# An early gather with more row buffers, and one tile's rows computed one stage earlier

## The chip, the cores and the metric

The kernel runs on one core of a Trainium2 chip. The time is the device time of one execution in microseconds. TensorE (PE) multiplies matrices, VectorE (DVE) and ScalarE (ACT) work on tiles of 128 partitions, GpSimd (POOL) does elementwise work and issues the indirect loads, SyncE (SP) issues plain loads. Each engine runs its own instructions strictly in the order in which they stand in its queue.

## The reference, cut to what matters

One layer of a decoder on 1024 prompt tokens and 64 sample tokens (8 sequences of 8), width 1024:

```python
xn = rmsnorm(h, norm_mix)
mix = token_mixers(xn, ...)            # one projection, retention heads and RWKV-7 heads, one output projection
h = h + mix
h = h + peer(rmsnorm(h, norm_ffn), peer_wq, peer_keys, peer_u, peer_v)
gate = sigmoid(rmsnorm(h, ple_norm) @ ple_gate)
h = h + gate * (p_l @ ple_proj)
```

`peer` is the part that the change is about. For each token it forms 8 query heads, scores two sets of 128 keys for each, takes the 16 best of each set and the 16 best sums, which gives 128 expert numbers out of 16384 and a softmax over each head's 16. Then

```python
hval = einsum('pd,phkd->phk', xb, u_tab[e])        # 128 rows of 1024 values for each token
act = gelu(hval) * gsm
y = einsum('phk,phkd->pd', act, v_tab[e])          # and 128 rows of the second table
```

All values are float32.

## The kernel before, in words

The 1088 tokens are nine tiles: 0 to 7 are the prompt, 128 tokens each, and 8 is the sample group, 64 tokens. The tiles differ in how `peer` is computed. Tiles 4 to 7 go through all 16384 experts densely (matmuls against both tables, with gates that are zero for experts not chosen). Tiles 0, 1 and 8 (`E0`) and 2 and 3 (`G1`) gather the chosen rows instead: for each of the 128 choices one indirect load fetches one row of 4 KB for each of the 128 partitions (the 64 tokens of tile 8 take two choices at a time), POOL issues it, and DVE works it off. In the first phase (table `pu`, line 1156) DVE multiplies the fetched rows with the token's row and sums them to one number; in the second (table `pv`, line 1170) it adds the scaled rows to a sum that is held in PSUM. In all there are 576 loads of each phase.

The stages, in the order of the program:

1. Projections of tiles 0 and 1 (group A0), then of 2 and 3 (group A1), beside the token mixing of tile 0.
2. Projections of tiles 4 to 8 (group A2). Here the early work begins: the output projection and norm of tile 0 (`c_rows`), its query (`early_query`), its choice of experts (`topk`) and its gather.
3. `group_b`: the token mixing of tiles 1, 8, 2, ..., 7, a chain of small matmuls, DVE and ACT steps, with the `c_rows` of the finished tiles and steps of the early work (queries and gathers of tiles 1 and 8) put between.
4. The handover: `c_rows` of the last tiles, the loads of the rows of tiles 2 to 7 and their transposes (`rows_in`, tile `cx`), then the queries of tiles 2 to 7 (`c_query`). What is left of the early gather runs on.
5. Choice of experts and gates of tiles 4 to 7 (`topk`, `gates`), beside 96 of the 128 blocks of the first dense product (`hidden`). The gathers of tiles 2 and 3 begin.
6. The dense product: the last 32 blocks fused, then the 96 stored ones.
7. The last part (`ple`): per-layer embedding, gate and final norm of tiles 0, 1, 8, 4, 5, 6, 7, 2, 3, in this order.

The order on each engine is set when the kernel is compiled: a scheduler takes the instructions in the program's order as their priority, runs a model of the engines' time, and places what is ready and comes first. So a gather that is late in the program stands early in an engine's queue where that model saw the engine free. Buffers bear a tag and a number of copies; a new tile of a tag waits until the oldest copy has been read.

The early work has one pool, `early`, laid out with the tags `V` (2 copies), `W` and `xy` (1 each), `Wq` (QB = 4) and `xT` (1), each 4 KB per partition. The rows of a gather take the tags of the tuple `rows` in turn, by `rows[j % len(rows)]` in `fetch`, so its length is the number of loads that can be under way or waiting for DVE. Before the change tiles 0 and 1 use `("V", "V", "W", "xy")`, four copies, and tile 8 uses these and `xT`, five. `Wq` holds the weight tiles of the queries of tiles 1 and 8, and at the end the second half of tile 7's mixed values (`tail`, line 984). Tiles 2 and 3 have a pool of their own (`grow`, five copies), which, with the buffers of the gates, lies where the early pool lay, and so waits for the end of the early gather.

Of the kernel before, what the change touches and what calls it, by code (L numbers as in the profile page):

```python
# [8 lines left out]
F32 = mybir.dt.float32  # L9
# [8 lines left out]
D = 1024  # L18
# [144 lines left out]
GBUF = 5  # L163
# [14 lines left out]
E0 = [0, 1, 8]  # L178
# [8 lines left out]
IB = 2  # L187
# [8 lines left out]
QB = 4  # L196
# [17 lines left out]
class K:  # L214
# [485 lines left out]
    def rw_mix(self, t):  # L700
        nc, I, O, wp = self.nc, self.I, self.O, self.cw
# [170 lines left out]
        V = toks["vtk"]  # L872
# [108 lines left out]
        p = self.ps("pgt", PGT or hb[0])  # L981
        nc.tensor.matmul(p[:n], sf13[:, :n], self.g2, start=True, stop=True)
        if t == 7:
            self.tail = self.ep0.tile([128, 512], F32, name="tail", tag="Wq", bufs=QB)
            nc.vector.tensor_tensor(self.tail, xf, p, op=OP.mult)
        else:
            nc.vector.tensor_tensor(xf[:n], xf[:n], p[:n], op=OP.mult)
            nc.scalar.dma_start(self.od[t][:n, 512:], xf[:n])
# [140 lines left out]
            nc.vector.tensor_scalar(e1[:n, 1], ei[:n], 127, None, op0=OP.bitwise_and)  # L1129
            nc.scalar.activation(self.e12[t][:n], e1[:n], AF.Copy)  # L1130

    def gather(self, gp, t, rows=("grow",), parts=1, acc=None):


        nc, I = self.nc, self.I
        n = SIZE[t]
        slot = lambda name, tag: gp.tile([128, D], F32, name=name, tag=tag, bufs=GBUF if len(rows) == 1 else 1 + (tag == "V"))
        home = lambda: acc.tile([128, 2, 512], F32, name="gacc", bufs=1).rearrange("p a b -> p (a b)")

        def fetch(src, j):  # L1140
# [20 lines left out]
        nc.scalar.activation(ac, hv[:, 0], AF.Gelu)  # L1161
        nc.vector.tensor_tensor(ac, ac, self.gsm[t], op=OP.mult)
        y = home()
        for j in range(n):
            g = fetch(I['pv'], j)
            for c in cs:
                if j == 0:
                    nc.vector.tensor_scalar(y[:, c], g[:, c], ac[:, 0:1], None, op0=OP.mult)
                else:
                    nc.vector.scalar_tensor_tensor(y[:, c], g[:, c], ac[:, j:j + 1], y[:, c], op0=OP.mult, op1=OP.add)  # L1170
            if j < n - 1:
                yield j
# [53 lines left out]
    def early(self, wp):  # L1226

        rows = ("V", "V", "W", "xy")
# [8 lines left out]
                yield  # L1237
        yield from g
        for t in E0[1:]:
            yield from self.gather(wp, t, rows + ("xT",) * (t == E0[-1]), acc=self.acc)  # L1240

    def gates(self, wp, t, extra):
        nc = self.nc
# [199 lines left out]
    def build(self):  # L1443
        PS = bass.MemoryType.PSUM
        run = lambda g: [None for _ in g]
        sb = lambda name, es, **kw: self.pool(name, es=es, reuse_waits="tile", **kw)
        with self.es:
# [15 lines left out]
            m = mix[0]  # L1463
            self.interleave(m, 1, a, IA)
            a = self.group_a(pools, A1, "b")
            self.interleave(m, IB, a, 1)
            e1.close()
            e0.close()
            self.ep0 = ep0 = sb("early", ee, side="right")
# [1 line left out]
            early = self.behind(self.early(ep0), PE_)  # L1471
            co = self.co = sb("co", ew, side="right")
            a = self.group_a(self.a_pool(e2, "2"), A2, "b")
            for _ in self.c_rows(co, E0[0]):
                next(a, None)
            for _ in a:
                for _ in range(IE):
                    next(early, None)
# [98 lines left out]
```

## Time and profile before

| | us |
|---|---|
| median of three runs | 3794.01 |
| lowest and highest | 3787.25 and 3801.23 |
| the profiled execution | 3785.29 |
| span of its trace | 3783.5 |

| engine | busy us | share of the span |
|---|---|---|
| PE | 3297.9 | 87% |
| DVE | 2964.3 | 78% |
| POOL | 2374.5 | 63% |
| ACT | 1227.5 | 32% |

The shares are means over stages with different limits, so they are read stage by stage. The profile's page cuts the span in 40 slices and gives each engine's busy share in tenths, the clock that PE was granted, and what the 16 DMA engines moved. The other views used below give the busy time of each engine in chosen stretches, who waited for whom, and single instructions in order of time.

### The profile page before, as it was taken

The numbers are of one execution on the slowest core, as the hardware profiler recorded it, in microseconds if no ns is written. First come the engines' busy times: TensorE is split into PE (matmuls) and PEld (weight loads), VectorE is DVE, ScalarE is ACT, GpSimd is POOL, SyncE is SP. The second block draws the span as 40 slices with busy tenths as digits, with TensorE's granted clock in tenths as the row PEclk, the third lists the DMA queues.
The fourth block names the chain that finished last, engine by engine and source line by source line (L and its number), as shares of the span: only waits on it lengthen the run. The fifth ranks groups of instructions, "written<-read, shape, count | busy, mean of one in ns | idle before, by whom it ended". The sixth has DMA issues, their size and how long they took to land. (4 is left out here: it accounts for less than half of the span.)

```text
span 3783.5 us, 52729 instructions
## 1 busy us (share of the span) xinstructions
PE 3297.9 (87%) x17749; PEld 2733.3 (72%) x17749; DVE 2964.3 (78%) x5858; ACT 1227.5 (32%) x2273; POOL 2374.5 (63%) x2059
## 2 busy tenths in 40 slices
PE   7799995858769978983999999999999989999979
PEld 7698994645648857762887777778788867777857
DVE  4454488978897798886998988997677878788886
ACT  4232221111112111211232635888433333333322
POOL 5363176445364456554559888775788778887752
PEclk9799995668867567876999999999999999999989
DMA  7266568889777878888779889898999999999984
GB/s 256 77 228 218 168 198 286 281 291 315 261 247 271 318 266 276 291 282 320 225 234 320 302 301 311 302 338 339 326 343 336 345 363 376 383 367 359 344 274 145
DMA packets 429898, 1086.24 MB, mean 287 GB/s; under 512 B 46972, under 2 KB 146042, under 8 KB 424955
## 3 DMA queue, kind: packets, MB, share of 16 engines
q0 software_dynamic: 165888, 604.05, 45.5%
q1 hardware_dynamic: 205406, 382.77, 30.9%
q10 hardware_dynamic: 58332, 96.03, 6.8%
q8 instruction: 141, 2.31, 0.3%
q14 instruction: 131, 1.07, 0.1%
HBM read 986.68 MB, written 95.94 MB: 286 GB/s over the span
## 5 line engine op out<-in xcount | busy, mean ns | idle before, releaser
L1142 POOL DMA_INDIRECT grow<-in_pv,eid x576 | 578.5, 1004 | 482.1 <-DVE gacc L1170 292.2
L1142 POOL DMA_INDIRECT grow<-in_pu,eid x576 | 569.7, 989 | 390.5 <-DVE grow L1156 213.4
L1170 DVE SCALAR_TENSOR_TENSOR gacc<-grow,ac,gacc 128x1024 f32<-128x1024 f32 x571 | 731.2, 1281 | 68.4 <-DMA grow<-in_pv,eid 63.4
L1156 DVE SCALAR_TENSOR_TENSOR grow<-grow,gacc 128x1024 f32<-128x1024 f32 x576 | 690.9, 1211 | 103.2 <-DMA grow<-in_pu,eid 101.2
L1317 PE MATMUL py<-ah,vh 128*128 128x512 f32 x1024 | 403.7, 396 | 29.2 <-ACT vh L299 29.0
L328 PE MATMUL ph<-cx,uh 128*128 128x512 f32 x1024 | 409.5, 400 | 21.3 <-ACT uh L299 14.9
L329 PE MATMUL ph<-cx,uh 128*128 128x512 f32 x1024 | 406.5, 397 | 0.0
L1318 PE MATMUL py<-al,vh 128*128 128x512 f32 x1024 | 402.0, 393 | 1.6 <-DVE al L301 1.6
L303 POOL TENSOR_TENSOR vl<-vraw,vh 128x640 fp32r<-128x640 f32 (+2 forms) x224 | 326.3, 1462 | 36.6 <-ACT vh L299 27.3
L303 POOL TENSOR_TENSOR ul<-uraw,uh 128x1024 fp32r<-128x1024 f32 x128 | 308.6, 2412 | 62.7 <-ACT uh L299 32.6
L1320 PE MATMUL py<-ah,vl 128*128 128x512 f32 x1024 | 270.9, 396 | 9.7 <-POOL vl L303 9.5
L331 PE MATMUL ph<-cx,ul 128*128 128x512 f32 x1024 | 261.1, 394 | 8.3 <-POOL ul L303 8.1
L1317 PEld LDWEIGHTS py<-ah,vh 128*128 128x128 f32 x1024 | 193.4, 189 | 81.1 <-ACT vh L299 38.8
L299 ACT ACTIVATE vh<-vraw 128x640 fp32r<-128x640 f32 (+2 forms) x224 | 154.8, 692 | 291.2 <-DMA vraw<-in_pvd 112.3
L328 PEld LDWEIGHTS ph<-cx,uh 128*128 128x128 f32 x1024 | 195.2, 191 | 67.6 <-ACT uh L299 20.7
L1320 PEld LDWEIGHTS py<-ah,vl 128*128 128x128 f32 x1024 | 191.8, 189 | 59.0 <-POOL vl L303 18.0
L1324 DVE TENSOR_TENSOR yT<-yT,py 128x512 f32<-128x512 f32 x216 | 147.3, 684 | 102.8 <-PE py L1320 101.2
L331 PEld LDWEIGHTS ph<-cx,ul 128*128 128x128 f32 x1024 | 189.7, 188 | 50.7 <-POOL ul L303 12.5
L1318 PEld LDWEIGHTS py<-al,vh 128*128 128x128 f32 x1024 | 193.5, 189 | 44.3 <-DVE al L301 2.9
L329 PEld LDWEIGHTS ph<-cx,uh 128*128 128x128 f32 x1024 | 194.9, 190 | 39.2
L299 ACT ACTIVATE uh<-uraw 128x1024 fp32r<-128x1024 f32 x128 | 135.4, 1058 | 188.8 <-DMA uraw<-in_puT 142.4
L303 POOL TENSOR_TENSOR wl<-wraw,wh 128x1024 fp32r<-128x1024 f32 x45 | 116.4, 2586 | 115.4 <-ACT wh L299 95.6
(402 smaller groups left out, 7456.4 us busy)
## 6 DMA issues: line engine op xcount, KB each, us to landing
uraw<-in_puT SPq DMA_DIRECT2D x128, 512.0 KB, 4.3
vraw<-in_pvd SPq DMA_DIRECT2D x152, 320.0 KB, 6.1
cw<-in_w_out SPq DMA_DIRECT2D x128, 256.0 KB, 5.1
wd<-wst ACTq DMA_DIRECT2D x28, 1024.0 KB, 17.7
wt<-wd SPq DMA_DIRECT2D x64, 448.0 KB, 7.1
wraw<-in_w_ret SPq DMA_DIRECT2D x48, 512.0 KB, 4.9
ewq<-in_wq SPq DMA_DIRECT2D x48, 512.0 KB, 7.3
gd<-geh ACTq DMA_DIRECT2D x96, 256.0 KB, 6.0
```

The costliest lines, as they stand in the source:

```text
L299: nc.scalar.activation(hi, src, AF.Copy)
L303: nc.gpsimd.tensor_tensor(lo, src, hi.bitcast(F32), op=OP.subtract)
L328: mm(out, lh(k), rh(k), start=first and k == 0, stop=False)
L329: mm(out, *((ll(k), rh(k)) if right else (lh(k), rl(k))), start=False, stop=False)
L331: mm(out, *((lh(k), rl(k)) if right else (ll(k), rh(k))), start=False, stop=last and k == nk - 1)
L1142: nc.gpsimd.indirect_dma_start(out=g, out_offset=None, in_=src, in_offset=bass.IndirectOffsetOnAxis(ap=self.eid[t][:, j:j + 1], axis=0))
L1156: nc.vector.scalar_tensor_tensor(g[:, c], g[:, c], 1.0, x[:, c], op0=OP.mult, op1=OP.mult, accum_out=hv[:, i, j:j + 1])
L1170: nc.vector.scalar_tensor_tensor(y[:, c], g[:, c], ac[:, j:j + 1], y[:, c], op0=OP.mult, op1=OP.add)
L1317: nc.tensor.matmul(p, vh[:, b, :], ah, start=b == 0, stop=False)
L1318: nc.tensor.matmul(p, vh[:, b, :], al, start=False, stop=False)
L1320: nc.tensor.matmul(p, vl[:, b, :], ah, start=False, stop=b == nb - 1)
L1324: nc.vector.tensor_tensor(yT[:, d, :], yT[:, d, :], p, op=OP.add)
```

## The change

Four edits. First, the rows of the second phase of tile 1's gather also take the four copies of `Wq` (8 in the ring), and tile 8's gather takes them in both phases, with `xT` (9 in the ring). Second, `tail` moves from `Wq` to `xT`, since `Wq` now belongs to the gather. Third, `c_rows` of tile 0 is no longer stepped at the start of group A2, but follows tile 0's mixing beside group A1, with a pool of its own (`co1`). Fourth, for that the two generators are joined in `then`.

```diff
@@ in rw_mix
         if t == 7:
-            self.tail = self.ep0.tile([128, 512], F32, name="tail", tag="Wq", bufs=QB)
+            self.tail = self.ep0.tile([128, 512], F32, name="tail", tag="xT")
@@ in gather
-    def gather(self, gp, t, rows=("grow",), parts=1, acc=None):
+    def gather(self, gp, t, rows=("grow",), parts=1, acc=None, more=()):
-        slot = lambda name, tag: gp.tile([128, D], F32, name=name, tag=tag, bufs=GBUF if len(rows) == 1 else 1 + (tag == "V"))
+        slot = lambda name, tag: gp.tile([128, D], F32, name=name, tag=tag, bufs=GBUF if len(rows) == 1 else dict(V=2, Wq=QB).get(tag, 1))
...
         y = home()
+        rows = rows + more
         for j in range(n):
             g = fetch(I['pv'], j)
@@ in early
         for t in E0[1:]:
-            yield from self.gather(wp, t, rows + ("xT",) * (t == E0[-1]), acc=self.acc)
+            if t == E0[-1]:
+                rows = rows + ("Wq",) * QB + ("xT",)
+            yield from self.gather(wp, t, rows, acc=self.acc, more=("Wq",) * QB if t != E0[-1] else ())
@@ in build
-            self.interleave(m, IB, a, 1)
+            e3 = ExitStack()
+            co = sb("co1", e3)
+
+            def then():
+                yield from m
+                yield from self.c_rows(co, E0[0])
+
+            self.interleave(then(), IB, a, 1)
+            e3.close()
...
             a = self.group_a(self.a_pool(e2, "2"), A2, "b")
-            for _ in self.c_rows(co, E0[0]):
-                next(a, None)
```

The scheduler then places many instructions anew. No engine gets an instruction more or less. Three places follow, on DVE each time; `grow` is a fetched row, `gacc` the sum in PSUM, so lines 1156, 1170 (1171 after the change) are the gather's.

In the last third of group A2's projections (`fdst` is the token shift of a projected block, `eid` the chosen experts of tile 0) there stood before:

```order
L559 SCALAR_TENSOR_TENSOR fdst<-fdst,vec,rs 128x64
L536 COPY rb<-shl 128x1
L541 COPY rs<-shiftT 128x8
L1099 TENSOR_REDUCE ef<-eq 128x16
L301 TENSOR_TENSOR wl<-wraw,wh 128x1024
L555 COPY shl<-rb 128x1
L1123 CAST eid_64<-ef 128x128
L560 COPY shl<-rs 128x8
L554 SCALAR_TENSOR_TENSOR fdst<-fdst,vec,rb 128x512
L559 SCALAR_TENSOR_TENSOR fdst<-fdst,vec,rs 128x64
```

and now, where the first of these blocks is shifted:

```order
L403 TENSOR_SCALAR gsig<-gsig 64x256
L1156 SCALAR_TENSOR_TENSOR grow,hv<-grow,gacc 128x1024
L404 TENSOR_TENSOR retd<-pret,gsig 64x256
L1156 SCALAR_TENSOR_TENSOR grow,hv<-grow,gacc 128x1024 x2
L301 TENSOR_TENSOR wl<-wraw,wh 128x1024
L555 COPY shl<-rb 128x1
L560 COPY shl<-rs 128x8
L1156 SCALAR_TENSOR_TENSOR grow,hv<-grow,gacc 128x1024
L554 SCALAR_TENSOR_TENSOR fdst<-fdst,vec,rb 128x512
L559 SCALAR_TENSOR_TENSOR fdst<-fdst,vec,rs 128x64
```

The experts of tile 0 were chosen between the fourth and fifth block; now the gather runs from the first block on. From the fifth block to the middle of tile 7's mixing, 8 to 18 more fetched rows, mostly 15, have been worked off ahead of each other DVE instruction than before.

At the handover (`ch` is the residual of `c_rows`, here of tile 7, `cx` the transposed rows of the tiles) there stood before:

```order
L301 TENSOR_TENSOR cx_13040<-ntr,cx_13039 128x4x128 x2
L1170 SCALAR_TENSOR_TENSOR gacc<-grow,ac,gacc 128x1024 x5
L609 TENSOR_TENSOR ch<-ewo,ch 128x512 x2
L1170 SCALAR_TENSOR_TENSOR gacc<-grow,ac,gacc 128x1024 x4
L629 SCALAR_TENSOR_TENSOR ch<-ch,crs,cgr 128x512 x2
L1170 SCALAR_TENSOR_TENSOR gacc<-grow,ac,gacc 128x1024
L301 TENSOR_TENSOR cx_13040<-ntr,cx_13039 128x4x128 x2
```

and now:

```order
L301 TENSOR_TENSOR cx_13098<-ntr,cx_13097 128x4x128 x2
L1171 SCALAR_TENSOR_TENSOR gacc<-grow,ac,gacc 128x1024 x5
L609 TENSOR_TENSOR ch<-ewo,ch 128x512
L1171 SCALAR_TENSOR_TENSOR gacc<-grow,ac,gacc 128x1024
L609 TENSOR_TENSOR ch<-ewo,ch 128x512
L1171 SCALAR_TENSOR_TENSOR gacc<-grow,ac,gacc 128x1024 x6
L1156 SCALAR_TENSOR_TENSOR grow,hv<-grow,gacc 128x1024 x2
L629 SCALAR_TENSOR_TENSOR ch<-ch,crs,cgr 128x512 x2
L1156 SCALAR_TENSOR_TENSOR grow,hv<-grow,gacc 128x1024
L301 TENSOR_TENSOR cx_13098<-ntr,cx_13097 128x4x128
```

Between the residual and the norm of tile 7 stand eight fetched rows in place of four, and the end of tile 1's gather and the start of tile 8's now fall there. Over the whole handover the lead grows from 15 rows to 37.

In the last part (`psg` the gate of `ple`, `fin` the final norm) there stood before, beside the gather of tile 3:

```order
L1170 SCALAR_TENSOR_TENSOR gacc<-grow,ac,gacc 128x1024
L1431 TENSOR_TENSOR psg<-psg,ppp 128x512
L301 TENSOR_TENSOR pxl<-ntr,pxh 128x512 x2
L1170 SCALAR_TENSOR_TENSOR gacc<-grow,ac,gacc 128x1024
L1440 SCALAR_TENSOR_TENSOR fin<-ph,frs,row_norm_final 128x512 x2
L1432 TENSOR_TENSOR ph<-ph,psg 128x512
L1170 SCALAR_TENSOR_TENSOR gacc<-grow,ac,gacc 128x1024
```

and now, about its last rows:

```order
L1171 SCALAR_TENSOR_TENSOR gacc<-grow,ac,gacc 128x1024
L1415 TENSOR_TENSOR ph<-ph,py 64x1024
L1435 TENSOR_TENSOR ph<-ph,psg 128x512
L1171 SCALAR_TENSOR_TENSOR gacc<-grow,ac,gacc 128x1024
L1431 TENSOR_SCALAR psg<-psg 128x512
L1171 SCALAR_TENSOR_TENSOR gacc<-grow,ac,gacc 128x1024
L313 SCALAR_TENSOR_TENSOR njunk<-ph,nrs,row_ple_norm 64x1024
L1434 TENSOR_TENSOR psg<-psg,ppp 128x512
L1443 SCALAR_TENSOR_TENSOR fin<-ph,frs,row_norm_final 128x512 x2
```

The last fetched row stood ahead of the eighth tile's sum with the gathered values (line 1412); it now stands ahead of the first final norm; until then the lead in this part is 24 rows. On PE the order from the handover to the last part is as before, but for the gates' matmuls (`pwt`), which from the second gated tile on stand up to 560 instructions earlier among those of `hidden`.

## The prediction

> **What bounds the kernel now.** I read the page's slices first, then the busy time by stage, then the waits of the stages in which PE stands still.
>
> ```profile
> span 3783.5 us, 52729 instructions
> ...
> PE 3297.9 (87%) x17749; PEld 2733.3 (72%) x17749; DVE 2964.3 (78%) x5858; ACT 1227.5 (32%) x2273; POOL 2374.5 (63%) x2059
> ...
> PE   7799995858769978983999999999999989999979
> ```
>
> A line is the whole span in 40 slices of 95 us. PE is short of work in many slices up to the nineteenth; from the twentieth on it is nearly full. So time lies in two places: the first half, where something else sets the pace, and what is left of PE's gaps later. The busy times by stage say how much. The columns are the stretch, its length, then busy time and instructions of PE, PE's weight loads, DVE, ACT and POOL, PE's granted clock, the DMA engines' busy share and GB/s.
>
> ```profile
> 243.00:300.00 57.00, 45.52 (x349) 43.91 (x347) 34.26 (x58) 23.34 (x36) 37.60 (x30) 0.91 0.75 253
> 300.00:440.00 140.00, 136.47 (x1065) 127.55 (x1066) 36.89 (x76) 33.10 (x71) 36.50 (x52) 0.99 0.71 226
> 440.00:577.00 137.00, 125.31 (x937) 122.88 (x935) 125.96 (x354) 31.76 (x70) 85.84 (x72) 0.98 0.56 180
> 577.00:1664.00 1087.00, 852.97 (x4683) 671.16 (x4684) 899.99 (x1770) 165.11 (x361) 571.40 (x563) 0.71 0.83 281
> 1664.00:1804.00 140.00, 80.45 (x409) 57.36 (x409) 95.13 (x105) 21.04 (x33) 63.09 (x64) 0.72 0.89 317
> 1804.00:2000.00 196.00, 193.28 (x1096) 168.86 (x1095) 191.00 (x913) 59.20 (x97) 111.04 (x90) 0.99 0.73 234
> 2000.00:2127.00 127.00, 115.28 (x509) 91.88 (x508) 106.73 (x292) 51.37 (x87) 114.14 (x82) 0.99 0.91 308
> 2127.00:2683.00 556.00, 522.09 (x2720) 438.94 (x2718) 486.57 (x832) 386.02 (x783) 421.21 (x309) 0.99 0.89 317
> 2683.00:3000.00 317.00, 312.73 (x1352) 255.77 (x1353) 244.24 (x303) 96.17 (x145) 263.41 (x216) 0.99 0.96 339
> 3000.00:3420.00 420.00, 384.08 (x1621) 304.57 (x1621) 338.04 (x596) 165.41 (x269) 341.88 (x284) 0.99 1.02 372
> ...
> 3640.00:3746.00 106.00, 104.75 (x490) 81.37 (x489) 95.08 (x120) 32.85 (x62) 48.87 (x55) 1.00 0.72 234
> 3746.00:3784.00 38.00, 28.53 (x126) 22.60 (x124) 16.88 (x25) 7.87 (x14) 3.93 (x8) 0.92 0.12 43
> ```
>
> In the mixing (577 to 1664) DVE is busy 900 of 1087 us and sets the pace. At the handover (1664 to 1804) PE stands for 60 of 140 us while DMA is busy to 0.89. From 1804 on PE is the limit; its gaps are 12 us up to 2127, 34 us up to 2683, 36 us in the stretch where DMA is full (1.02), and hardly 1 us from 3640 to 3746.
>
> ```profile
> L1142 POOL DMA_INDIRECT grow<-in_pv,eid x576 | 578.5, 1004 | 482.1 <-DVE gacc L1170 292.2
> L1142 POOL DMA_INDIRECT grow<-in_pu,eid x576 | 569.7, 989 | 390.5 <-DVE grow L1156 213.4
> L1170 DVE SCALAR_TENSOR_TENSOR gacc<-grow,ac,gacc 128x1024 f32<-128x1024 f32 x571 | 731.2, 1281 | 68.4 <-DMA grow<-in_pv,eid 63.4
> L1156 DVE SCALAR_TENSOR_TENSOR grow<-grow,gacc 128x1024 f32<-128x1024 f32 x576 | 690.9, 1211 | 103.2 <-DMA grow<-in_pu,eid 101.2
> ```
>
> These price a fetched row: 1.0 us of POOL, 1.2 to 1.3 us of DVE, and, at 128 x 4 KB, 0.52 MB. They also say what a longer ring can buy. POOL waits long for DVE to free a buffer, but DVE, which the mixing needs, waited for rows only 68 + 103 us in the whole run. A ring hides that part alone; it takes no DVE work away.
>
> **The change part by part.** I counted in the two orders how many fetched rows stand ahead of the same other DVE instruction. The lead of the new order is 15 rows where the mixing begins and still 15 at 1664 us, 37 at 1804, 38 at 2000, 47 at 2127, 30 at 2683, 25 at 3000 and 3420, 24 at 3640, and 0 at the end. So each stage gains or loses the difference: group A2 +15, mixing 0, handover +22, queries +1, then +9, -17, -5, 0, and -24 in the last part. Each is priced by who is short there.
>
> *Tile 0's rows beside group A1.* The move shifts PE work, and brings the first row forward.
>
> ```profile
> L616 PE MATMUL ewo<-cw,coT x32: 590/592/594, 321.3 to 346.0; 128*128 128x512 f32 x32
> ...
> L988 ACTq DMA_DIRECT2D od<-hnx x1: 326/326/326, 247.2 to 247.2; - x1
> ...
> L1142 POOL DMA_INDIRECT grow<-in_pu,eid x44: 936/942/1680, 523.2 to 619.9; - x44
> ```
>
> 32 x 0.592 = 19 us of matmuls move from group A2, where PE stood only 3.5 us between 300 and 440, to A1's end, where it stood 11.5 us of 57. The mixed values are stored at 247, so the work can start there. What fills a gap is won, at most 11 us; the rest changes places. SP's 16 weight loads and the other loads of `c_rows` move too, past those of group A2, into a stretch with DMA at 0.75. A matmul that waits there holds A1's projections behind it. The nearest row for such a wait is the one of 17.5 us below, with 4 MB of other loads around it; I take half as the bound, +8. I take -4 (-11 to +8).
>
> *15 rows more in group A2*, 15 x 1.29 = 19 us of DVE (1.21 and the read-out of the sum). Between 300 and 440 DVE has 103 us free, and what stood at 440 (tile 0's choice of experts) moves there; PE sets the pace. I take 0; without that cover DVE would have 126 + 19 us of work in 137, +8. The mixing keeps its DVE work and its order, 0 (-6 to +6: a lead of 8 to 18 instead of 15 moves some 5 rows of 1.2 us about).
>
> *The handover, 22 rows more.* These rows carry the argument.
>
> ```profile
> PE ntr L322 <- DMA cxn<-xd: 17.5, 1, 17.5
> ...
> PE ntr L322 <- issue: 13.7, 1, 13.7
> PE ntr L322 <- DVE cx L301: 9.2, 2, 8.6
> ...
> 1734.16 1.29 DVE L1170 SCALAR_TENSOR_TENSOR gacc<-grow,ac,gacc 128x1024 f32<-128x1024 f32 x1 [3.28 <-DMA grow<-in_pv,eid]
> ...
> 1795.66 1.29 DVE L1170 SCALAR_TENSOR_TENSOR gacc<-grow,ac,gacc 128x1024 f32<-128x1024 f32 x1 [4.38 <-DMA grow<-in_pv,eid]
> 1796.86 1.41 DVE L629 SCALAR_TENSOR_TENSOR ch<-ch,crs,cgr 128x512 f32<-128x512 f32 x2
> ```
>
> Here the longer ring helps: at 1734 and 1795 DVE stood for a row that had not landed, with the transposed rows and tile 7's norm behind it, and PE behind these. With eight rows under way instead of four both waits can go, -8 us. Against it: DVE has 45 us free and gets 22 x 1.28 = 28 us more, partly on the same chain, since eight rows now stand between tile 7's residual and its norm, with the change from tile 1's sum to tile 8's among them. And 22 rows are 11.5 MB more. The stretch moved 317 GB/s x 140 us = 44 MB; the highest rate of a long stretch is 372 GB/s, by which 56 MB need 150 us: +10. That is nearest to what binds PE there, a load of rows and weights, so I take +10 (-8 to +28).
>
> The Trainium skill (DMA: Bandwidth & Descriptors, "Where 436 GB/s comes from") gives a core about 358 GB/s of HBM; by it the 56 MB would take 156 us and the term be +16. The 372 GB/s of this trace lie above, some of them writes, and the measurement decides. The same page ("Queues, rings and completion order") says that each DMA engine goes round its queues packet by packet, so that a longer gather queue takes no larger share from SP's loads; by that rule the term would fall toward 0, and no row here shows it.
>
> *The queries* get one row, +1. *2000 to 2127* gets nine: 9 us more of POOL, busy 114 of 127, and POOL also makes the low halves (`ul`) that PE waits for. PE has 12 us of gaps; I take +4 (0 to +9). *2127 to 2683* loses 17 rows, 22 us of DVE, 17 of POOL.
>
> ```profile
> PE pwt L1266 <- ACT oh L1263: 15.2, 12, 2.9
> PE ph L328 <- ACT uh L299: 14.9, 11, 2.5
> PE ph L331 <- POOL ul L303: 8.1, 8, 2.5
> ```
>
> These are PE's waits from 2000 to 2683. The gates' matmuls also start earlier, since the early pool is free sooner, so ACT's work for them spreads. Gates wait on ACT, dense blocks on ACT and POOL, none directly on a fetched row, so of the 22 us I take half and a little, -12 (-34, all gaps, to 0).
>
> *The dense product* loses five rows where PE is 99% busy and none where DMA is full: 0 (-4 to 0). *The last part* loses 24 rows, 31 us of DVE. But PE is busy 104.8 of 106 us there, so they were hidden. At the very end tile 3 no longer waits for its gather; PE worked 28.5 of the last 38 us, and part of the rest lies behind its last matmul: -2 (-6 to 0).
>
> The sum is -4 + 0 + 0 + 10 + 1 + 4 - 12 + 0 - 2 = -3 us, from 3785.3 us of the profiled execution (its span and 1.8 us around it) to 3782. The three runs have their median at 3794.0, 8.7 us above that execution, so I say 3791.
>
> **The rivals.** *The relief pays.* If the waits for rows at the handover cover most of its new work (+2), the front wins 6, the gates all 22 us and the end 4, the change is 30 us: 3764. For it: DVE is 88% busy from 2127 to 2683, and every gather row gone there is one less ahead of an `oh`. Against it: PE is 94% busy there, and PE's own waits name ACT.
>
> *The handover gets longer.* All 22 rows stand on the path: +28, and POOL's nine in 2000 to 2127 fall on PE, +9, with -4 and -2 kept and the gates' relief lost because the gates only start as much later: 3825. It decides from 15 of the 22 rows on (15 x 1.28 = 19 us). For it: PE waits for DVE and DMA there and nothing covers it. Against it: DVE's 45 free us.
>
> *The ring does nothing.* If DVE's order, not the buffers, paces the gather on the chip, then waits and lead stay as they are and only the front's -4 is left: 3790.
>
> A rule that would speak for a gain is that of the Trainium skill (Perfetto Trace Analysis, "Optimization Strategy"): the same gap repeated on the engine that should be full can mean too few buffers. By it the 8 us of row waits at the handover are won, and more where such waits stand later, which is the first rival; PE's gaps there have three different causes in the rows above.
>
> **How the numbers follow.** The near-cancelling sum has 0.48, the paying relief 0.24, the longer handover 0.16, the idle ring 0.12. 0.5% is 19 us, about what a measurement of this kernel can tell from no change. Faster than that: 0.20 of the first rival and 0.06 of the sum's lower tail, 0.26. Slower: 0.14 of the second and 0.04, 0.18. The same: 0.56. The range reaches from just past the first rival, 3762, to near the second, 3820.
>
> **What would show it.** Right: the first row fetched at about 475 us, PE at the end of group A2 within 5 us of before; the mixing as long as before; a handover of 145 to 155 us with few waits of DVE for rows and more DMA than 317 GB/s; tile 8's gather done some 40 rows sooner, the stretch to 2683 some 10 us shorter; the last row consumed by about 3665. Wrong: a mixing that is more than 15 us longer or shorter; a handover under 135 us; or PE's gaps after 2127 halved.

## The result, and the profile after

The change made the kernel slower: the median went from 3787.7 us to 3803.9 us (22 runs of each). The ratio of the runs, with one slow run of before, at 4690 us, left out, is 1.0052 with a 95% interval of 1.0035 to 1.0068, which is 13 to 26 us. The forecast was 3 us faster. The profiled execution of the change took 3793.0 us against 3785.3 before, so it shows 8 us of the loss. A second profile of the same kernel, below, shows 14.6.

The page of the changed kernel, as shown of before: the span, the busy times, and PE's share in 40 slices.

```profile
span 3791.1 us, 52718 instructions
...
PE 3290.4 (87%) x17749; PEld 2724.8 (72%) x17749; DVE 2962.5 (78%) x5858; ACT 1225.8 (32%) x2273; POOL 2356.3 (62%) x2059
...
PE   7798995868769879883998899999999988899979
```

The work is the same and PE's busy time is 7.5 us less, so in sum the loss is waiting. The busy times by stage say where. The borders follow the work (the same matmul in both traces) to about 2 us: at the handover PE's order changed by a dozen matmuls, and from the same transpose on (1658.08 us, not 1656) it is 3 us longer and not 5. Inside 1997 to 2688 two kinds of matmuls changed places; there the border is set so that PE's busy time agrees, and another one is tried below.

```profile
303.50:446.00 142.50, 121.86 (x968) 118.96 (x969) 67.44 (x271) 35.60 (x74) 43.78 (x66) 0.92 0.64 201
446.00:584.00 138.00, 131.06 (x1002) 129.67 (x1001) 115.56 (x192) 32.47 (x72) 96.46 (x81) 0.99 0.73 240
584.00:1656.00 1072.00, 843.29 (x4685) 659.14 (x4686) 903.72 (x1753) 163.79 (x361) 577.25 (x567) 0.71 0.84 286
1656.00:1801.00 145.00, 78.08 (x405) 55.16 (x404) 121.15 (x131) 21.59 (x34) 84.01 (x86) 0.73 1.01 388
...
1997.00:2140.00 143.00, 115.44 (x486) 92.42 (x485) 131.55 (x283) 51.06 (x87) 115.82 (x89) 0.92 0.87 300
2140.00:2688.00 548.00, 521.33 (x2736) 442.49 (x2735) 459.88 (x835) 384.87 (x783) 401.44 (x289) 0.99 0.84 304
```

| stage (before) | before | after | difference | forecast |
|---|---|---|---|---|
| up to the end of group A2 (577) | 577 | 584 | +7 | -4 |
| mixing (to 1664) | 1087 | 1072 | -15 | 0 |
| handover (to 1804) | 140 | 145 | +5 | +10 |
| queries (to 2000) | 196 | 196 | 0 | +1 |
| first dense blocks (to 2127) | 127 | 143 | +16 | +4 |
| rest of the gates (to 2683) | 556 | 548 | -8 | -12 |
| dense product (to 3640) | 957 | 962 | +5 | 0 |
| last part | 143.5 | 141 | -2.5 | -2 |

The largest loss is the stretch of 127 us that now needs 143, with 115 us of PE's busy time in both. PE's waits there (first two rows, from 1801 to 2140) name POOL, and so do the single rows (in brackets: how long the engine stood before the row, and what ended it):

```profile
PE ph L331 <- POOL ul L303: 20.8, 5, 6.7
PE ph L328 <- ACT uh L299: 6.3, 3, 3.1
...
2074.78 3.68 PE L331 MATMUL ph<-cx,ul 128*128 128x512 f32 x8 [4.29 <-POOL ul L303]
2094.17 3.78 PE L331 MATMUL ph<-cx,ul 128*128 128x512 f32 x8 [6.63 <-POOL ul L303]
2114.57 3.78 PE L331 MATMUL ph<-cx,ul 128*128 128x512 f32 x8 [6.72 <-POOL ul L303]
```

Before, from 1804 to 2127, PE waited 3.1 us for `ul` and 8.3 us for `uh`. The waits are not the whole price. The eight `ul` matmuls of a block took 3.7 us behind each of these three waits; before the change, where nothing holds them, they take 2.0 us:

```profile
2042.82 1.98 PE L331 MATMUL ph<-cx,ul 128*128 128x512 f32 x8
```

So equal busy time is not equal work, and a border by the work is fairer. Here are the same twelve dense blocks (96 matmuls with `ul` each), before and after.

```profile
2047.00:2128.00 81.00, 72.08 (x333) 57.59 (x332) 64.25 (x150) 36.44 (x67) 73.15 (x54) 1.00 0.90 302
```

```profile
2045.00:2151.00 106.00, 81.71 (x361) 66.11 (x361) 95.40 (x154) 44.32 (x85) 86.34 (x69) 0.90 0.88 308
```

They take 25 us longer (26 in the second profile). About 14 us are waits for `ul` and `uh` (23.0 us after 8.9), 6 us are the `ul` matmuls (30.2 us after 24.1, at a granted clock of 0.90 after 1.00), and 4 us are matmuls of the gates that now stand here (80 after 48) and are missing later. What POOL did between two `ul` shows the rest. First POOL's queue in order of time before the change, then after it:

```profile
2085.61 2.39 POOL L303 TENSOR_TENSOR ul<-uraw,uh 128x1024 fp32r<-128x1024 f32 x1
2087.95 1.75 POOL L1098 TENSOR_TENSOR eq<-eq,eid 128x800 f32<-128x800 f32 x1
2089.86 0.98 POOL L1142 DMA_INDIRECT grow<-in_pv,eid  x1 [0.16 <-issue]
2091.15 0.94 POOL L1142 DMA_INDIRECT grow<-in_pv,eid  x1 [0.30 <-issue]
2092.11 2.40 POOL L303 TENSOR_TENSOR ul<-uraw,uh 128x1024 fp32r<-128x1024 f32 x1
```

```profile
2091.76 2.36 POOL L303 TENSOR_TENSOR ul<-uraw,uh 128x1024 fp32r<-128x1024 f32 x1
2094.28 1.53 POOL L1142 DMA_INDIRECT grow<-in_pv,eid  x1 [0.16 <-issue]
2096.11 0.94 POOL L1142 DMA_INDIRECT grow<-in_pv,eid  x1 [0.30 <-issue]
2097.35 0.94 POOL L1142 DMA_INDIRECT grow<-in_pv,eid  x1 [0.30 <-issue]
2098.60 0.94 POOL L1142 DMA_INDIRECT grow<-in_pv,eid  x1 [0.30 <-issue]
2099.56 1.79 POOL L1098 TENSOR_TENSOR eq<-eq,eid 128x800 f32<-128x800 f32 x1
2101.51 0.98 POOL L1142 DMA_INDIRECT grow<-in_pv,eid  x1 [0.16 <-DVE gacc L1171]
2102.51 2.39 POOL L303 TENSOR_TENSOR ul<-uraw,uh 128x1024 fp32r<-128x1024 f32 x1
```

Two fetches between two low halves became five, at 1.25 us from one to the next, and the distance from `ul` to `ul` went from 6.5 to 10.8 us. Each dense block needs one `ul`. POOL hardly waits for a buffer here ("issue" is time in which it waited for nothing that the profile shows), so it is busy with the fetches themselves. The extract shows the longest gap. Over the ten gaps from 2031 to 2121 us the mean is 9.0 us with 42 fetches; over ten from 2033 to 2099 before the change it was 6.6 us with 24. Their order is fixed when the kernel is compiled: nine copies let it put five in a row, with five copies it never put more than three in this part.

### The profile page after: what moved, and what is told of

It reads as the page before. It is cut to its first block, busy times and chain, and to the rows that moved or that the text cites. A ratio compares the mean times of both kernels' runs of the same rounds, so it can differ in the third digit from the quotient of the medians.

```text
span 3791.1 us, 52718 instructions
## 1 busy us (share of the span) xinstructions
PE 3290.4 (87%) x17749; PEld 2724.8 (72%) x17749; DVE 2962.5 (78%) x5858; ACT 1225.8 (32%) x2273; POOL 2356.3 (62%) x2059
## 5 line engine op out<-in xcount | busy, mean ns | idle before, releaser
L1142 POOL DMA_INDIRECT grow<-in_pv,eid x576 | 570.3, 990 | 403.8 <-DVE gacc L1171 249.1
L331 PE MATMUL ph<-cx,ul 128*128 128x512 f32 x1024 | 269.4, 401 | 20.9 <-POOL ul L303 20.8
L1264 DVE TENSOR_TENSOR oh<-csta,pit 128x512 f32<-128x512 f32 x256 | 161.8, 678 | 19.9 <-PE pwt L1269 8.0
```

What stands on the lines that cost most here:

```text
L331: mm(out, *((lh(k), rl(k)) if right else (ll(k), rh(k))), start=False, stop=last and k == nk - 1)
L1142: nc.gpsimd.indirect_dma_start(out=g, out_offset=None, in_=src, in_offset=bass.IndirectOffsetOnAxis(ap=self.eid[t][:, j:j + 1], axis=0))
L1264: nc.vector.tensor_tensor(oh[:, j], io, p[:, j, s + b:s + b + 4, None].to_broadcast([128, 4, 128]), op=OP.is_equal)
```

## The experiments

My theory after this reading: the longer ring of tile 8 lets the order on POOL put four or five fetches ahead of each `ul`, and PE waits for these low halves. The rivals: tile 0's rows beside group A1 are the cause, or the added rows at the handover. "Lead" is the number of fetches ahead of the first dense block's `ul` in POOL's order, less that of before (525).

### One part at a time

Each kernel is the one before with one part of the change. Only the moved `c_rows`, with rings and `tail` as before:

```diff
-            self.interleave(m, IB, a, 1)
+            self.interleave(then(), IB, a, 1)
...
-            for _ in self.c_rows(co, E0[0]):
-                next(a, None)
```

> Only tile 0's c_rows moves beside group A1; rings and tail stay as before. Theory (the ring of tile 8 bunches the fetches on POOL between two low halves ul, and PE waits for ul between 2000 and 2140): about the time of before, at most 7 us slower, since the front of the whole change stood 7 us later at the end of group A2 and the mixing gave it back; POOL's order here has 2 to 3 fetches between two ul as before, so PE should wait under 8 us for ul from 2000 to 2140. Rival 1 (the front is the cause: loads and matmuls of c_rows hold group A1): 15 to 20 us slower, like the whole change. Rival 2 (more rows at the handover are the cause): same as before.

Both rings and the moved `tail`, with `c_rows` of tile 0 in group A2 as before:

```diff
+            if t == E0[-1]:
+                rows = rows + ("Wq",) * QB + ("xT",)
+            yield from self.gather(wp, t, rows, acc=self.acc, more=("Wq",) * QB if t != E0[-1] else ())
```

> Both rings and the tail in xT, but c_rows of tile 0 stays in group A2. Theory (bunched fetches): 10 to 20 us slower than before, with PE waiting about 20 us for POOL's ul between 2000 and 2140, since POOL's order has again 4 to 5 fetches between two ul there. Rival 1 (the front): same as before. Rival 2 (handover): 10 to 20 us slower, but with the handover 10 us longer and PE's waits for ul below 10 us.

Tile 1's ring alone:

```diff
+            yield from self.gather(wp, t, rows + ("xT",) * (t == E0[-1]), acc=self.acc, more=("Wq",) * QB if t != E0[-1] else ())
```

> Only tile 1's second phase gets the eight-row ring (tail in xT); tile 8 keeps five rows. POOL's order has a lead of about 28 fetches at the first dense block, like the whole change (39), but 2 to 3 fetches between two ul, as before. Theory (bunched fetches): no slower than before, possibly 5 to 10 us faster, since the waits for rows at the handover go and the gates start sooner. Rival 2 (more rows at the handover, whatever comes behind): 10 to 20 us slower. Rival 1: same as before.

Tile 8's ring alone:

```diff
+            if t == E0[-1]:
+                rows = rows + ("Wq",) * QB + ("xT",)
+            yield from self.gather(wp, t, rows, acc=self.acc)
```

> Only tile 8's gather gets the nine-row ring (tail in xT); tile 1 keeps four rows. POOL's order has no lead at the first dense block (2 fetches), but up to 6 fetches between two ul in the first 17 dense blocks, and again 5 to 7 in every second gap from block 31 on. Theory (bunched fetches): 10 to 25 us slower than before, PE waiting 15 us or more for ul between 2000 and 2300. Rival 2 (handover): same as before. Rival 1 (front): same as before.

Measured, as ratios to before with their 95% intervals: the front alone 1.0028 (1.0005 to 1.0051), both rings 1.0045 (1.0023 to 1.0066), tile 1's ring alone 0.9964 (0.9944 to 0.9983), tile 8's ring alone 1.0070 (1.0040 to 1.0101). So the two rings have opposite signs: tile 1's is a gain of 14 us, tile 8's a loss of 26 us. The rival of the handover falls as the cause of the whole loss: tile 1's ring brings 29 rows of lead and the kernel gets faster, though the handover of its profile is 151 us for 140. The front is a smaller loss of its own, 11 us (2 to 19), more than the 7 us that I allowed it.

One expectation missed in form. With both rings PE waited only 8.4 us for `ul` in the first dense blocks, not 20, but 18.7 us for `uh`:

```profile
PE ph L328 <- ACT uh L299: 18.7, 8, 3.2
PE ph L331 <- POOL ul L303: 8.4, 3, 5.4
...
ACT uh L299 <- DMA uraw<-in_puT: 46.5, 10, 7.4
...
SPq L1282 <- POOL ul L303: 195.5, 26, 11.4
```

The third row is ACT's own wait, for the load of the block's rows (`uraw`), and the last is SP's, which issues these loads: all 26 from 1971 to 2180 us waited for a `ul`. `uraw` has two copies (`UB`), each held until POOL has made the block's `ul` from it, so a late `ul` also delays the load after it and with it `uh`. ACT's wait alone is no measure of the loss: before the change it is longer (88 us in the first 190 us of the dense blocks), and PE waited little. Both of PE's waits together are the measure: 27 us with both rings and 27 us in the whole change, against 11 us before.

### The ring's length, and POOL's part in it

Tile 8's ring of seven rows instead of nine, tile 1's as in the change, `c_rows` as before:

```diff
-                rows = rows + ("Wq",) * QB + ("xT",)
+                rows = rows + ("Wq",) * 2 + ("xT",)
```

> Both rings as in the change, but tile 8's ring has seven rows instead of nine (two of the four Wq copies); c_rows of tile 0 stays in group A2. POOL's order has 3 to 4 fetches between two low halves ul where the nine-row ring has 4 to 5 and the five-row ring 2 to 3. Theory (bunched fetches on POOL): between the five-row ring, which was 14.6 us faster than before, and the nine-row ring, 18.5 us slower: -5 to +12 us. Rival (it is not the ring's length but that tile 8 takes Wq at all, or the tail in xT): like the nine-row ring, 18 us slower.

The whole change with the low halves of the first 24 dense blocks on DVE, and the same edit in the kernel before as a control:

```diff
-        self.split(uh, ul, raw, "g")
+        self.split(uh, ul, raw, "v" if i1 < 24 else "g")
```

> The whole change, but the low halves ul of the first 24 dense blocks are made by DVE instead of POOL, so that no fetch on POOL stands ahead of them. Theory (PE waits for POOL's ul behind bunched fetches): PE's waits for POOL's ul between 2000 and 2140 fall from 21 us to under 5, and the time falls by 8 to 20 us against the change, to 3784 to 3796. DVE gets 24 x 1.3 = 31 us more work, of which up to 10 us may come back as PE waiting for DVE. Rival (the loss lies in the front and in DVE's order at the handover): no faster than the change, 3804 or above.

> The control of the run with DVE's low halves: the kernel before with the same edit. There POOL has 2 to 3 fetches between two ul and PE waited only 3 us for them up to 2127. Theory (bunched fetches): at most 5 us faster, rather 0 to 10 us slower by DVE's 31 us of added work; so the gap between the change and before, 16 us without the edit, shrinks to under 8 us with it. Rival: the gap stays 16 us.

The change without tile 8's nine-row ring (it keeps five):

```diff
-            if t == E0[-1]:
-                rows = rows + ("Wq",) * QB + ("xT",)
-            yield from self.gather(wp, t, rows, acc=self.acc, more=...)
+            yield from self.gather(wp, t, rows + ("xT",) * (t == E0[-1]), acc=self.acc, more=...)
```

> Tile 0's c_rows beside group A1 and tile 1's eight-row ring, tile 8 at five rows: the change without the nine-row ring of tile 8. Theory (the nine-row ring costs about 30 us, the rest of the change is good or neutral): between 15 us faster (tile 1's ring alone) and the same as before, by what the front costs: it stood 7 us later at the end of group A2, so about 7 us faster than before. Rival (the front alone costs 14 us, as its own run shows): no faster than before, 0 to +3 us.

Measured: seven rows 1.0013 (0.9990 to 1.0035), between five and nine as the theory wants. (The seven are the length of the tuple; `Wq` keeps its four copies, so two of the seven can run ahead by a turn.) The change with DVE's 24 low halves 1.0014 (0.9990 to 1.0038), its control 1.0029 (1.0010 to 1.0048): with POOL out of the way the change is no longer slower than its control. But the absolute gain is small (its median, 3801.1 us, misses the 3784 to 3796 that was expected), since both kernels got a new wait in one place, where DVE was late with the first `ul`s:

```profile
PE ph L331 <- DVE ul L301: 30.4, 1, 30.4
```

```profile
PE ph L331 <- DVE ul L301: 23.0, 1, 23.0
```

The first row is of the change with the edit, the second of its control. The front with tile 1's ring came to 1.0003 (0.9983 to 1.0022), where tile 1's ring alone had 0.9964: the front takes the whole gain away, 15 us, as its rival had it.

So the next run moves only the low halves of blocks 12 to 23 to DVE, the ones that POOL's order has behind four and five fetches:

```diff
-        self.split(uh, ul, raw, "g")
+        self.split(uh, ul, raw, "v" if 12 <= i1 < 24 else "g")
```

> The whole change, but only the low halves ul of dense blocks 12 to 23 are made by DVE, the blocks before which POOL's order of the change has four to five fetches each; the first twelve, where DVE was late by 30 us in the run with 24, stay on POOL. Theory (PE waits for ul behind bunched fetches): PE's waits for any ul between 2000 and 2140 fall from 21 us to under 8, and the time by 8 to 20 us against the change's 1.0052, to a ratio of 1.000 to 1.003. Rival (the front and the dense product carry the loss): 1.005 as before the edit.

Measured: 0.9971 (0.9944 to 0.9997), better than expected. PE's waits for `ul` and `uh` in the first 190 us of the dense blocks fell from 27 us to the 2.8 us of this row:

```profile
PE ph L331 <- POOL ul L303: 2.8, 2, 2.0
```

and the stage from the first dense block to the end of the gates from 738 to 711 us. The twelve blocks above take 90 us in it. That is the most direct test: the change with everything in it, and only the low halves of twelve blocks taken from behind POOL's fetches, is 0.6% faster than without by the medians (3782.6 and 3803.9 us) and 0.8% by the two ratios. The scheduler placed other instructions anew as well, and POOL lost 12 x 2.4 = 29 us of work, so whether the bunches or POOL's load pay is left to the last run below.

Below five rows, and the next gather's ring (both with tile 1's eight rows and `c_rows` as before):

```diff
-            yield from self.gather(wp, t, rows + ("xT",) * (t == E0[-1]), acc=self.acc, more=...)
+            yield from self.gather(wp, t, rows, acc=self.acc, more=...)
```

> As the run with tile 1's ring alone, but tile 8's ring has four rows instead of five. POOL's order has 1 to 3 fetches between two ul, a little under 2 on average in the first 24 gaps, against 2 to 3 with five rows. Theory (a shorter ring paces the fetches and only its bunching costs): 0.9964 or a little better, 0.993 to 0.998, unless DVE's waits for rows grow by more than 10 us, which would show there. Rival (the gain of tile 1's ring alone comes from tile 8's gather ending sooner, and a shorter ring undoes it): 0.998 to 1.002.

```diff
-GBUF = 5
+GBUF = 4
```

> As the run with tile 1's ring alone, but the gathers of tiles 2 and 3 have four row buffers instead of five. The order of the first dense blocks is that of tile 1's ring alone; later POOL has up to nine fewer fetches ahead of block 96. Theory (longer rings bunch fetches ahead of the low halves, wherever PE waits for POOL): as good as tile 1's ring alone or up to 5 us better, 0.995 to 0.9965. Rival (five rows are needed where DMA is full, from 3000 on): 10 us or more slower than tile 1's ring alone, DVE waiting more for rows there.

The changed kernel as it is, for a second profile:

> The changed kernel once more, unaltered, for a second profile. If the stage differences belong to the order of instructions, the front is again 5 to 10 us longer up to the end of group A2, PE waits again about 20 us for POOL's ul between 2000 and 2140, and the stage from the first dense block to the end of the gates is again some 10 us longer than before; the mixing, 14 us shorter in the first profile, may come out as long as before, since it differed by 21 us between two kernels whose orders are the same up to there.

Measured: four rows for tile 8 0.9937 (0.9909 to 0.9965), the fastest kernel of the study, 24 us faster than before. Four row buffers for tiles 2 and 3 1.0050 (1.0021 to 1.0079), as the rival had it, but not where it looked. The stored dense product even got shorter, and the end longer. Of before, then of this kernel:

```profile
3000.00:3640.00 640.00, 577.77 (x2449) 459.59 (x2449) 517.25 (x826) 235.03 (x388) 501.82 (x424) 0.97 1.00 360
3640.00:3783.00 143.00, 133.29 (x614) 103.97 (x612) 111.96 (x145) 40.72 (x76) 52.80 (x63) 0.98 0.56 185
```

```profile
2996.00:3609.00 613.00, 573.75 (x2450) 462.40 (x2449) 472.35 (x790) 234.01 (x388) 466.78 (x388) 0.97 0.98 345
3609.00:3806.00 197.00, 137.09 (x614) 106.28 (x612) 151.10 (x176) 40.96 (x76) 80.86 (x95) 0.86 0.65 219
...
PE ntr L322 <- DVE njunk L313: 48.1, 1, 48.1
```

The dense product has thirty-six fewer fetches (388 instructions of POOL instead of 424) and is 27 us shorter, where DMA is full. But the last row was consumed at 3768 instead of 3733 us, and PE stood 48 us for the last norm behind it, a wait that the kernel before does not have. Here a short ring paces the gather past the time at which it must be done.

The second profile of the change has a span of 3798.0 us. Its stages against before: +6 us up to the end of group A2, -1 in the mixing, +4 in the handover (+3 from the same transpose to the same matmul of the queries), +5 from the first dense block to the end of the gates, +3 in the dense product, -2 in the last part. The waits in the first dense blocks are there again, 22.6 us for `ul` and 4.7 for `uh`. The 15 us that the first profile had won in the mixing are gone. They were not the change's: the kernel before and the control with DVE's low halves have the same order on every engine up to the end of the mixing. Of before the row is the prediction's (1087 us from 577 to 1664); this is the control's:

```profile
580.00:1646.00 1066.00, 836.36 (x4682) 655.91 (x4682) 891.56 (x1767) 164.66 (x361) 572.15 (x563) 0.72 0.84 285
```

Twenty-one us between two executions of the same order, in a stretch that the change hardly touches, are more than the effect in question. With the mixing set aside, the two profiles of the change show 22 and 15 us of loss, both within the interval of the ratio.

### What was still open

Whether the four rows gain by themselves, whether it goes on below four, and whether POOL's load as such is the limit. First the kernel before with tile 8's ring at four rows and nothing else:

```diff
-            yield from self.gather(wp, t, rows + ("xT",) * (t == E0[-1]), acc=self.acc)
+            yield from self.gather(wp, t, rows, acc=self.acc)
```

> The kernel before with one edit: tile 8's ring has four rows instead of five; tile 1's stays at four. POOL's order has an even 2 fetches between two ul in the first 24 gaps, with a lead of 6 fetches at the first dense block. Theory (the ring's length sets the pace of the fetches, and with it how long PE waits for POOL and ACT): faster by a third to a half of what both edits gave (0.9937), 0.996 to 0.999. Rival (the gain comes from tile 1's rows, whose lead of 28 at the first dense block lets the gates start sooner): 0.999 to 1.003.

Then tile 1's eight rows with three rows for tile 8:

```diff
-            yield from self.gather(wp, t, rows + ("xT",) * (t == E0[-1]), acc=self.acc, more=...)
+            yield from self.gather(wp, t, rows[1:] if t == E0[-1] else rows, acc=self.acc, more=...)
```

> Tile 1's second phase with eight rows, tile 8's ring with three. The series so far: nine rows 1.0045, seven 1.0013, five 0.9964, four 0.9937. POOL's order has 1.8 fetches between two ul instead of 2.1. Theory (fetches bunched on POOL are the cost): it flattens, 0.992 to 0.996, since PE waited only 3 us for ul with four rows. Rival (fewer rows are better throughout): 0.990 or less. If rows come late, DVE's waits for rows of tile 8 grow by over 15 us and the ratio goes back above 0.997.

And the fastest kernel (eight rows for tile 1, four for tile 8) with DVE's low halves of blocks 12 to 23:

```diff
-        self.split(uh, ul, raw, "g")
+        self.split(uh, ul, raw, "v" if 12 <= i1 < 24 else "g")
```

> Tile 1's second phase with eight rows, tile 8 with four, and the low halves ul of dense blocks 12 to 23 made by DVE. Theory (bunching is the cost; with four rows it is gone, PE's waits for ul are 3 us): no further gain, 0.992 to 0.996, as DVE pays 16 us for what POOL saves. Rival (POOL's load as such is the limit up to the end of the early gather): 5 to 10 us better than with four rows alone, 0.989 to 0.991.

Measured: 1.0052 (1.0031 to 1.0073), 1.0006 (0.9985 to 1.0027) and 0.9980 (0.9958 to 1.0001). All three miss. The whole-kernel ratio is too coarse here, because other stages move with every new order. So this is the stage itself, from the first dense block to the end of the gates; waits are PE's for `ul` and `uh` in its first 190 us:

| kernel | rows of tile 1, second phase | rows of tile 8 | stage us | waits us | ratio |
|---|---|---|---|---|---|
| tile 8's ring alone | 4 | 9 | 757 | 16.7 | 1.0070 |
| before | 4 | 5 | 728 | 11.4 | 1 |
| tile 8 shorter | 4 | 4 | 729 | 4.1 | 1.0052 |
| both rings | 8 | 9 | 743 | 27.1 | 1.0045 |
| | 8 | 7 | 733 | 20.8 | 1.0013 |
| tile 1's ring alone | 8 | 5 | 710 | 9.9 | 0.9964 |
| the fastest | 8 | 4 | 706 | 3.0 | 0.9937 |
| | 8 | 3 | 718 | 5.1 | 1.0006 |
| front alone | 4 | 5 | 720 | 7.2 | 1.0028 |
| the change, two profiles | 8 | 9 | 738, 733 | 27.1, 27.3 | 1.0052 |
| the change, 12 low halves on DVE | 8 | 9 | 711 | 2.8 | 0.9971 |
| the fastest, 12 low halves on DVE | 8 | 4 | 700 | 0.0 | 0.9980 |
| front with tile 1's ring | 8 | 5 | 710 | 9.7 | 1.0003 |
| tile 1's ring, 4 buffers for tiles 2 and 3 | 8 | 5 | 724 | 8.3 | 1.0050 |

The rows behind three lines of the table, before, tile 8 at nine rows alone, and the fastest kernel:

```profile
1959.00:2687.00 728.00, 678.36 (x3407) 564.78 (x3405) 636.89 (x1314) 449.24 (x887) 566.91 (x418) 0.99 0.89 314
```

```profile
1966.00:2723.00 757.00, 690.36 (x3409) 575.85 (x3407) 647.94 (x1339) 448.86 (x888) 585.89 (x439) 0.96 0.88 318
```

```profile
1962.00:2668.00 706.00, 674.54 (x3406) 565.18 (x3405) 617.20 (x1291) 447.57 (x888) 557.37 (x407) 0.99 0.89 315
```

Each stage time is from one profile. The two of the change differ by 5 us, so smaller steps of the table are not resolved. (In the ring of three, `V` keeps two copies, so one of the three can run ahead by a turn.)

In the stage the picture holds. Going from five rows to nine for tile 8 costs 29 to 33 us, whatever tile 1 has. (With tile 1 at four rows only 5 us of it are waits for `ul` and `uh` in the first 190 us; 12 us are PE's own time, 690 us for the same matmuls that took 678, at a granted clock of 0.96 for 0.99.) Tile 1's ring pays 14 to 23 us at each length of tile 8's, because tile 8's last fetch is then issued at 2212 us (tile 8 at five rows) instead of 2289, and the gates of the second gated tile start some 70 us sooner. At three rows the stage gets longer again. Rows that come late are not the reason, since DVE's waits for them hardly grew (156 us in the whole run, 153 with four rows); tile 8's last fetch is issued at 2282 us (2238 with four rows), and the gates of the second gated tile wait for the end of the early gather. The last run also answers whether the bunches or POOL's load pay: taking the same twelve low halves from POOL shortens the stage by 27 and 22 us in the change, where fetches are bunched, and by 6 us in the fastest kernel, where they are not.

The whole time does not follow the stage everywhere. With four rows for tile 8 and four for tile 1 the stage is as long as before, yet the kernel is 0.5% slower. Its profile shows the loss in the stored dense product, where DMA is full: 660 us instead of 640, at 348 GB/s instead of 360. The run with four rows and DVE's low halves has the shortest stage of all, 700 us, and 659 us there. What lowers the rate I have not settled; the amount moved is the same (660 x 348 and 640 x 360, both 230 MB). The other kernels with five buffers for tiles 2 and 3 lie between, at 641 to 655 us, so this stage alone differs between kernels by as much as the change cost.

## Why the prediction was wrong

**The step that failed is the price of the rows between 2000 and 2127**, +4 us (0 to +9), and with it the judgement that the longer ring of tile 8 is free on POOL. I counted nine more fetches at 1.0 us each and set them against PE's 12 us of gaps. Measured was +16 us, or +25 over the same twelve dense blocks: 14 us of waits, 6 us of matmuls that ran slower and 4 us of gates' work moved forward. Up to the end of the gates, -8 us was forecast in sum (+4 and -12), and +8 and +5 us were measured. What counts there is not how many fetches POOL issues in the stage but how many stand in a row ahead of one `ul`: five at 1.25 us and an `eq` of 1.8 us make 10.8 us from `ul` to `ul`. I had the row that should have warned me, POOL busy 114 of 127 us before the change, and I had the order of the changed kernel, in which the bunches stand; I read from it only the lead.

**The front** failed too, in sign: -4 us (-11 to +8) was forecast, and +7 and +6 us stand at the end of group A2, up to 3 us of which the kernels without the move show as well; in the whole time the runs with and without it differ by 11 and 15 us. (In the presence of the nine-row ring they differ by 3 us, 1.0052 against 1.0045, within their intervals.) The gaps at A1's end were filled as I said, but a new one opened behind them. Of the change, SP's queue at that place (L240 and L353 are the first loads of group A2's norm, L615 and L628 those of `c_rows`), and PE's wait:

```profile
278.86 3.50 SPq L615 DMA_DIRECT2D cw<-in_w_out  x3
285.12 0.33 SPq L530 DMA_DIRECT2D wraw<-in_w_rw  x1
285.71 1.54 SPq L628 DMA_DIRECT2D cgr<-in_rows  x2
290.65 0.33 SPq L240 DMA_DIRECT2D row_norm_mix<-in_rows  x1
...
294.59 8.60 SPq L353 DMA_DIRECT2D x<-in_x  x2
...
PE ntr L322 <- DVE njunk L313: 9.5, 1, 9.5
```

Before, these two loads were issued at 250.4 and 252.0 us. I had the loads moved "past those of group A2" and priced a wait in A1; it was group A2 whose first norm had its loads issued 40 us later, behind the 16 weight loads. Why the order puts it there was not tried. The rest of the front's 11 to 15 us seems to lie elsewhere: the profiles (one of each) of the front alone and of the front with tile 1's ring have some 10 us more in the stored dense product (650 us for 640, and 655 for 645 with tile 1's ring alone). The change does not have them (645 and 644, with both rings and no front 651), so that part depends on the rest of the order, and its cause stays open.

**The handover** was right in sign and about a third to a half as large, +3 to +5 us in both profiles for +10. (Its length scatters between kernels: 151 us with tile 1's ring alone, 141 in the fastest kernel, and 150 with four rows for both, where tile 1's ring is the old one.) DVE's waits for rows went from 20.4 to 8.0 us, as argued, and the added rows moved. PE's 14.1 us behind tile 7's `tail` fell to 3.1, but a wait of 11.8 us behind a fetched row on DVE (`gacc`) is new. The transfers cost less than I priced them: I divided 56 MB by 372 GB/s, the highest rate in my rows, and the stretch moved them at 388 GB/s (397 in the second profile). DMA is busy to 1.01 there, so it is not shown whether the transfers or DVE's order set the +3 to +5 us. The Trainium skill's figure (DMA: Bandwidth & Descriptors, "Where 436 GB/s comes from"), about 358 GB/s of HBM for a core (a stack's 716 divided between two), would have made it +16 by my estimate. The 388 GB/s, in which writes are counted too, lie above it, with one core at work, and the measurement decides. The same page ("Queues, rings and completion order") says that each DMA engine goes round its queues packet by packet. What I took from that, that a longer gather queue takes no larger share from the other loads and the term falls toward 0, agrees with the +3 to +5 us better than my +10, but no run here separates the queues.

**Group A2, the mixing and the queries** came as forecast, once the mixing's own scatter of 20 us is known. "Wrong if the mixing is more than 15 us longer or shorter" was too sharp a test for one profile.

**2127 to 2683** gave -8 for -12: the early pool was free sooner and the gates started sooner, as said. Tile 8's last fetch is issued at 2141 us in the change and at 2289 before. Both rings bring it forward, tile 1's alone to 2212 and tile 8's alone to 2254, but only tile 1's shortens the stage by itself, by 18 us; the nine rows lose more ahead of the gates than they win by them.

**The dense product and the last part**: +5 and -2.5 us for 0 and -2. The 24 rows of lead into the last part won nothing, as argued. Two readings of mine were short: PE's gaps from 1804 to 2127 are 14 us, not 12, and I showed no row for 3420 to 3640, where PE is busy 194 of 220 us. The +5 us do not lie there, but between 3000 and 3420 (426 us for 420).

Of the rivals, *the handover gets longer* named the price (POOL's rows falling on PE up to 2127, +9) but hung it on the wrong place. The rule from the Trainium skill (Perfetto Trace Analysis, "Optimization Strategy") that a repeated gap can mean too few buffers does not hold here: the repeated gap on PE, 4.3, 6.6 and 6.7 us at every second block, came with more buffers.

## What to carry to other kernels

A ring of buffers is also a brake on the engine that fills it: where that engine has other work on a critical path in the same queue, count how many fills the new length lets stand in a row ahead of that work, and price the row, not the sum. Here eight rows paid for tile 1, whose rows run ahead before the dense blocks begin, and nine rows cost for tile 8, whose fetches run beside the dense blocks' low halves on the same engine. When one change has several parts, time each alone before believing the sum: here a gain of 14 us and losses of 26 and 11 us were in one edit.

## What was not expected of the hardware

A stretch of 140 us moved 388 to 397 GB/s with DMA busy to 1.01 and 1.02, where before the best 140 us after 1500 (3100 to 3240) moved 380. Behind a wait of 4.3 to 6.7 us PE's next eight matmuls took 3.7 us where they otherwise take 2.0; what sets this was not tried. And two executions of the same order differ by 21 us in the mixing alone, 1087 and 1066 us, with the same clock to 0.01 (0.71 and 0.72), DVE's busy time 900 and 892 us, and the DMA rate 281 and 285 GB/s; what makes the difference was not tried.
